# Softmax on one core: VectorE scales every row by its own scalar, ScalarE scales none

## The chip, the core and the metric

The kernel runs on one core of a Trainium2 chip. The engines that work here are VectorE (DVE in the profile), ScalarE (ACT), GpSimd (POOL) and SyncE (SP); SP, ACT and POOL also issue transfers, each into queues of its own, and the core's 16 DMA engines carry them. TensorE is idle. The metric is the device time of one execution in microseconds (us); lower is better. The kernel before takes 161.75 us, the median of 3 runs (161.74 to 161.76).

## What is computed

The input is a float32 tensor of 16 x 1024 x 512, 33.55 MB; the output has the same shape. It is a softmax over the last axis with temperature 0.5:

```python
x_scaled = x / 0.5
x_max = np.max(x_scaled, axis=-1, keepdims=True)
exp_x = np.exp(x_scaled - x_max)
return exp_x / np.sum(exp_x, axis=-1, keepdims=True)
```

## The kernel before

The 16384 rows of 512 elements are cut into 8 chunks of 2048 rows. A chunk is a tile `xt` of 128 partitions by 16 rows by 512 elements, 4 MB (4.19 million bytes). There are six such buffers (`BUFS = 6`), so chunk 6 uses chunk 0's buffer again, and chunk 7 chunk 1's. Everything is computed in place in the buffer.

*Transfers.* `load(c)` (L61, the transfer on L68) loads a chunk on SP's queue. Chunk 0 comes in two pieces of 4 and 12 rows, chunks 1 to 6 whole, and chunk 7 without its last row. That row is loaded by `load_last_row` (L88) on POOL's queue, as soon as a copy (L90) has seen ScalarE's sum of row 10 of chunk 5. The loads of chunks 0 to 5 wait for nothing but the queue; those of chunks 6 and 7 wait until stores 0 and 1 have landed. `store(i)` (L144, the transfer on L148) stores a whole chunk and is issued on ScalarE's queue, once all 16 rows have been scaled.

*Compute.* A chunk is worked on in blocks (`BLOCKS`): chunk 0 in blocks of 4, 4 and 8 rows, chunks 1 to 6 in one block of 16, chunk 7 in two of 8; 11 blocks in all. For one block:

- `shift(i)` (L71), VectorE: the negative row maxima of the whole block in one reduction (L77), then one tiny multiply by 2 gives the biases (L81).
- `exponentials(i, rows)` (L102), ScalarE: one activation per row (L108), exp(2x + bias), which also gives the row's sum.
- `scale_vector(i)` (L120), VectorE: the reciprocals of the block's sums (L125), and one multiply of the first seven eighths of the block's rows by them, the reciprocals being broadcast along each row (L127).
- `scale_scalar(i)` (L133), ScalarE: the last eighth of the rows, one activation per row (L138), Copy with the reciprocal as the per-partition scale. This is two rows of a block of 16, one of a block of 8, none of a block of 4.

*Order.* The schedule is written out by hand: each engine runs its instructions in the order in which the program names them. The loop over blocks (L163) names, for block i: the exponentials of block i+1 (for chunk 1 all but the last two rows), `scale_vector(i)`, `scale_scalar(i)`, the maxima and biases of block i+2, the store if the block ends a chunk, and then the rows of block i+1 that were left out. So VectorE alternates between scaling a block and reducing the block after next, and its next scale waits for ScalarE's exponentials of that block; ScalarE's exponentials wait for VectorE's biases. At the very end SP waits for what is listed in `finished` (L174).

Of the kernel before, what the change touches and what calls it, by code (L numbers as in the profile page):

```python
# [1 line left out]

# [4 lines left out]


@with_exitstack
def kernel(  # L10
    ctx: ExitStack,
    tc: tile.TileContext,
    x: bass.AP,
    out: bass.AP,
):
    nc = tc.nc
    fp32 = mybir.dt.float32
    P = nc.NUM_PARTITIONS
    AX = mybir.AxisListType.X
    EXP = mybir.ActivationFunctionType.Exp  # L20
    COPY = mybir.ActivationFunctionType.Copy
    MAX = mybir.AluOpType.max

    D = x.shape[-1]
    xf = x.flatten_outer_dims()
    of = out.flatten_outer_dims()
    N = xf.shape[0]

    G = 16
    C = N // (P * G)
    assert C * P * G == N
    xr = xf.rearrange("(c p g) d -> c p g d", p=P, g=G)
    outr = of.rearrange("(c p g) d -> c p g d", p=P, g=G)
    WHOLE = [(0, G)]
    LOADS = [[(0, 4), (4, G)]] + [WHOLE] * 6 + [[(0, G - 1)]]
    BLOCKS = [[(0, 4), (4, 8), (8, G)]] + [WHOLE] * 6 + [[(0, 8), (8, G)]]
    STORES = [WHOLE] * 8  # L40
    BMAX = 16
    BUFS = 6

    data = ctx.enter_context(tc.tile_pool(name="data", bufs=BUFS))
    stats = ctx.enter_context(tc.tile_pool(name="stats", bufs=6))

    ctx.enter_context(tc.manual_schedule())


    warm = stats.tile([P, 1], fp32, name="warm", bufs=1)  # L50
    nc.vector.memset(warm, 0.0)  # L51
    nc.scalar.activation(out=warm, in_=warm, func=EXP)  # L52

    chunks = {}
    blocks = [(c, lo, hi) for c in range(C) for lo, hi in BLOCKS[c]]
    n = len(blocks)
    biases, sums, recips = {}, {}, {}

    finished = []

    def load(c):  # L61
        if c < BUFS:
            chunks[c] = data.tile([P, G, D], fp32, name="xt")
        else:
            chunks[c] = chunks[c - BUFS]
        xt = chunks[c]
        for lo, hi in LOADS[c]:
            part = nc.sync.dma_start(out=xt[:, lo:hi, :], in_=xr[c][:, lo:hi, :])  # L68
            finished.append(part.ins.name)

    def shift(i):  # L71
        c, lo, hi = blocks[i]
        if c not in chunks:
            load(c)
        b = hi - lo
        negmax = stats.tile([P, BMAX], fp32, name="negmax")
        nc.vector.tensor_reduce(  # L77
            negmax[:, 0:b], chunks[c][:, lo:hi, :], axis=AX, op=MAX, negate=True
        )
        biases[i] = stats.tile([P, BMAX], fp32, name="bias")  # L80
        nc.vector.tensor_scalar_mul(biases[i][:, 0:b], negmax[:, 0:b], 2.0)  # L81

    def load_last_row(signal):  # L88
        seen = stats.tile([P, 1], fp32, name="seen", bufs=1)
        copied = nc.gpsimd.tensor_copy(out=seen, in_=signal)  # L90
        finished.append(copied.ins.name)
        c = C - 1
        halves = "p (h d) -> p h d"
        to = chunks[c - BUFS][:, G - 1, :].rearrange(halves, h=2)
        of_ = xr[c][:, G - 1, :].rearrange(halves, h=2)
        for p0, p1 in ((P - 2, P), (0, P - 2)):
            part = nc.gpsimd.dma_start(  # L97
                out=to[p0:p1], in_=of_[p0:p1], max_dma_last_dim=2 * D
            )
            finished.append(part.ins.name)  # L100

    def exponentials(i, rows):  # L102
        c, lo, hi = blocks[i]
        if i not in sums:
            sums[i] = stats.tile([P, BMAX], fp32, name="sums")
        for g in rows:
            row = chunks[c][:, lo + g, :]
            nc.scalar.activation(  # L108
                out=row,
                in_=row,  # L110
                func=EXP,
                bias=biases[i][:, g : g + 1],
                scale=2.0,
                accum_out=sums[i][:, g : g + 1],
            )
            if c == BUFS - 1 and g == 10:
                load_last_row(sums[i][:, g : g + 1])


    def scale_vector(i):  # L120
        c, lo, hi = blocks[i]
        b = hi - lo
        k = b - b // 8
        recips[i] = stats.tile([P, BMAX], fp32, name="recip")
        nc.vector.reciprocal(recips[i][:, 0:b], sums[i][:, 0:b])  # L125
        rows = chunks[c][:, lo : lo + k, :]
        last = nc.vector.tensor_mul(  # L127
            rows, rows, recips[i][:, 0:k].unsqueeze(2).broadcast_to((P, k, D))
        )
        if i == n - 1:  # L130
            finished.append(last.ins.name)

    def scale_scalar(i):  # L133
        c, lo, hi = blocks[i]
        b = hi - lo
        for g in range(b - b // 8, b):
            row = chunks[c][:, lo + g, :]
            last = nc.scalar.activation(  # L138
                out=row, in_=row, func=COPY, scale=recips[i][:, g : g + 1]
            )  # L140
            if i == n - 1:
                finished.append(last.ins.name)

    def store(i):  # L144
        c, _, end = blocks[i]
        for lo, hi in STORES[c]:
            if hi == end:
                part = nc.scalar.dma_start(  # L148
                    out=outr[c][:, lo:hi, :], in_=chunks[c][:, lo:hi, :]
                )  # L150
                if c < C - 1:
                    finished.append(part.ins.name)

    shift(0)
    shift(1)

    def rows(i):
        c, lo, hi = blocks[i]
        cut = hi - lo - (2 if c == 1 else 0)
        return range(cut), range(cut, hi - lo)  # L160

    exponentials(0, rows(0)[0])
    for i in range(n):  # L163
        if i + 1 < n:
            exponentials(i + 1, rows(i + 1)[0])
        scale_vector(i)
        scale_scalar(i)
        if i + 2 < n:
            shift(i + 2)
        store(i)  # L170
        if i + 1 < n:
            exponentials(i + 1, rows(i + 1)[1])

    seen = nc.sync.nop()  # L174
    info = mybir.DependencyInfo(
        mybir.DependencyClass.Sync, mybir.DependencyReason.DATA
    )
    for name in finished:
        tc.add_manual_dep(seen.ins, name, info, reason="leaves one wait for the end")


# [1 line left out]
_INS = ['x']  # L183
_OUTS = [((16, 1024, 512), 'float32')]


# [23 lines left out]
```

## Time and profile before

| quantity | value |
| --- | --- |
| median of 3 runs | 161.75 us |
| span of the profiled execution, first to last instruction | 160.5 us |
| VectorE busy | 134.6 us, 84% of the span, 45 instructions |
| ScalarE busy | 102.2 us, 64%, 273 instructions |
| DMA, whole span | 67.13 MB, mean 418 GB/s |
| a 16-row block on VectorE: maxima (L77) / scale of 14 rows (L127) | 8.68 / 7.62 us |
| a row on ScalarE: exponential (L108) / scale (L138) | 708 / 706 ns |

The page gives the span of the profiled execution; its time is not listed beside those of the three runs. Those lie 1.25 us above the span: what comes before the first instruction and after the last. 

When a store or a late load is issued, and when it lands (issue and time to landing are the trace's, the landing is their sum):

| transfer | issued, us | to landing, us | landed, us |
| --- | --- | --- | --- |
| store of chunk 0 | 44.10 | 24.5 | 68.6 |
| store of chunk 1 | 58.95 | 28.9 | 87.9 |
| store of chunk 2 | 75.57 | 31.4 | 107.0 |
| store of chunk 3 | 92.18 | 28.8 | 121.0 |
| store of chunk 4 | 108.81 | 21.7 | 130.5 |
| store of chunk 5 | 125.43 | 14.8 | 140.2 |
| store of chunk 6 | 133.00 | 17.0 | 150.0 |
| store of chunk 7 | 147.48 | 12.2 | 159.7 |
| load of chunk 6 | 68.67 | 27.6 | 96.3 |
| load of chunk 7, rows 0 to 14 | 88.02 | 27.8 | 115.8 |
| load of chunk 7, last row (POOL, two pieces) | 104.82 | 9.1 and 15.4 | about 120.9 |

How to read the profile's lines: a group of instructions is given as line, engine, operation, output and input with their shapes (partitions x elements) and a count; then busy time in us, the mean duration of one in ns, and the engine's idle time just before them with what ended it. A line of a timeline begins with start and duration in us. A line of busy times by stretch gives the stretch, its length, the busy time of VectorE, ScalarE and POOL in it, TensorE's granted clock, the share of the 16 DMA engines that was busy (packets are counted where they start, so short stretches can exceed 1), and GB/s. A line of a DMA queue gives packets, MB, and the time that its packets took as a share of 16 engines; q1 holds SP's loads, q10 ScalarE's stores, q0 POOL's load.

### The profile page before, as it was taken

The numbers are of one execution on the slowest core, as the hardware profiler recorded it, in microseconds if no ns is written. First come the engines' busy times: TensorE is split into PE (matmuls) and PEld (weight loads), VectorE is DVE, ScalarE is ACT, GpSimd is POOL, SyncE is SP. The second block draws the span as 40 slices with busy tenths as digits, with TensorE's granted clock in tenths as the row PEclk, the third lists the DMA queues.
The fourth block names the chain that finished last, engine by engine and source line by source line (L and its number), as shares of the span: only waits on it lengthen the run. The fifth ranks groups of instructions, "written<-read, shape, count | busy, mean of one in ns | idle before, by whom it ended". The sixth has DMA issues, their size and how long they took to land.

```text
span 160.5 us, 411 instructions
## 1 busy us (share of the span) xinstructions
DVE 134.6 (84%) x45; ACT 102.2 (64%) x273; POOL 1.9 (1%) x7
## 2 busy tenths in 40 slices
DVE  0607999999999999999999999999999999957000
ACT  3071549069989963998199909991899891790000
POOL 0000000000000000000000000030000000000000
DMA  5999999999989999999999999989999999999994
GB/s 184 470 408 498 400 392 457 457 392 402 506 269 425 490 392 400 506 400 392 490 425 392 474 434 392 490 383 483 422 450 400 400 465 441 392 457 449 400 441 204
DMA packets 2578, 67.13 MB, mean 418 GB/s; under 512 B 328, under 2 KB 328, under 8 KB 400
## 3 DMA queue, kind: packets, MB, share of 16 engines
q1 hardware_dynamic: 1296, 33.29, 49.3%
q10 hardware_dynamic: 1152, 33.55, 48.4%
q0 software_dynamic: 128, 0.26, 0.4%
q14 instruction: 2, 0.02, 0.0%
HBM read 33.55 MB, written 33.55 MB: 418 GB/s over the span
## 4 chain that ended last, share of the span: by engine, by line
DVE 75%; DMA 7%; issue 5%; ACT 3%; SPq 0%
DVE negmax L77 42%; DVE xt L127 31%; DMA xt<-in_x_dram 7%; ACT xt L108 3%; DVE bias L81 1%; DVE recip L125 1%; SPq L68 0%
## 5 line engine op out<-in xcount | busy, mean ns | idle before, releaser
L108 ACT ACTIVATE xt<-xt,bias 128x512 f32<-128x512 f32 x128 | 90.4, 708 | 41.5 <-DVE bias L81 40.6
L77 DVE TENSOR_REDUCE negmax<-xt 128x16 f32<-128x8192 f32 (+2 forms) x11 | 69.9, 6352 | 9.4 <-DMA xt<-in_x_dram 9.4
L127 DVE TENSOR_TENSOR xt<-xt,recip 128x7168 f32<-128x7168 f32 (+2 forms) x11 | 62.0, 5637 | 0.4
L108 ACT ACTIVATION_READ_ACCUMULATOR xt<-xt,bias 128x1 f32 x128 | 23.9, 187 | 0.0
L138 ACT ACTIVATE xt<-xt,recip 128x512 f32<-128x512 f32 x15 | 9.9, 706 | 0.0
L125 DVE RECIPROCAL recip<-sums 128x16 f32<-128x16 f32 (+2 forms) x11 | 2.4, 218 | 1.8 <-ACT xt L108 1.8
L81 DVE TENSOR_SCALAR bias<-negmax 128x16 f32<-128x16 f32 (+2 forms) x11 | 1.9, 173 | 0.4
L52 ACT ACT_TABLE_LOAD x1 | 1.3, 1283 | 0.7 <-PEq L194 0.7
L97 POOL DMA_DIRECT2D xt<-in_x_dram x2 | 1.5, 741 | 0.5 <-issue 0.5
L90 POOL COPY seen<-sums 128x1 f32<-128x1 f32 x1 | 0.2, 184 | 103.6 <-ACT xt L108 103.6
L51 DVE MEMSET warm<- 128x1 f32 x1 | 0.1, 59 | 0.8 <-PEq L194 0.8
L52 ACT ACTIVATE warm<-warm 128x1 f32<-128x1 f32 x1 | 0.2, 202 | 0.0
L194 POOL MEMSET const-float32-0.0<- 128x1 f32 x1 | 0.1, 93 | 0.2 <-issue 0.2
L194 POOL MEMSET const-bfloat16-1.0<- 128x1 bf16 x1 | 0.1, 95 | 0.0
L194 POOL MEMSET const-uint8-127<- 128x1 uint8 x1 | 0.1, 95 | 0.0
L194 POOL MEMSET const-float32-1.0<- 128x1 f32 x1 | 0.1, 93 | 0.0
## 6 DMA issues: line engine op xcount, KB each, us to landing
out_dram<-xt ACTq DMA_DIRECT2D x8, 4096.0 KB, 23.1
xt<-in_x_dram SPq DMA_DIRECT2D x6, 4096.0 KB, 34.8
xt<-in_x_dram SPq DMA_DIRECT2D x1, 3840.0 KB, 27.8
xt<-in_x_dram SPq DMA_DIRECT2D x1, 3072.0 KB, 11.6
xt<-in_x_dram SPq DMA_DIRECT2D x1, 1024.0 KB, 4.8
xt<-in_x_dram POOLq DMA_DIRECT2D x1, 252.0 KB, 15.4
xt<-in_x_dram POOLq DMA_DIRECT2D x1, 4.0 KB, 9.1
```

What stands on the lines that cost most here:

```text
L51: nc.vector.memset(warm, 0.0)
L52: nc.scalar.activation(out=warm, in_=warm, func=EXP)
L77: nc.vector.tensor_reduce(negmax[:, 0:b], chunks[c][:, lo:hi, :], axis=AX, op=MAX, negate=True)
L81: nc.vector.tensor_scalar_mul(biases[i][:, 0:b], negmax[:, 0:b], 2.0)
L90: copied = nc.gpsimd.tensor_copy(out=seen, in_=signal)
L97: part = nc.gpsimd.dma_start(out=to[p0:p1], in_=of_[p0:p1], max_dma_last_dim=2 * D)
L108: nc.scalar.activation(out=row, in_=row, func=EXP, bias=biases[i][:, g : g + 1], scale=2.0, accum_out=sums[i][:, g : g + 1],)
L125: nc.vector.reciprocal(recips[i][:, 0:b], sums[i][:, 0:b])
L127: last = nc.vector.tensor_mul(rows, rows, recips[i][:, 0:k].unsqueeze(2).broadcast_to((P, k, D)))
L138: last = nc.scalar.activation(out=row, in_=row, func=COPY, scale=recips[i][:, g : g + 1])
L194: nc = _bacc.Bacc("TRN2", target_bir_lowering=False, num_devices=1)
```

## The change

VectorE's one broadcast multiply per block is replaced by one multiply per row, whose second operand is a per-partition scalar, the row's reciprocal; it covers all rows of the block. ScalarE scales no rows. The reciprocal, the order of the loop and all transfers stay as they are named; `finished` is created some lines earlier, without effect. The lines of the code after move up by a few (the row multiply is L126 there, the store L134).

```diff
-    def scale_vector(i):
+    def scale(i):
         c, lo, hi = blocks[i]
         b = hi - lo
-        k = b - b // 8
         recips[i] = stats.tile([P, BMAX], fp32, name="recip")
         nc.vector.reciprocal(recips[i][:, 0:b], sums[i][:, 0:b])
-        rows = chunks[c][:, lo : lo + k, :]
-        last = nc.vector.tensor_mul(
-            rows, rows, recips[i][:, 0:k].unsqueeze(2).broadcast_to((P, k, D))
-        )
+        for g in range(b):
+            row = chunks[c][:, lo + g, :]
+            last = nc.vector.tensor_scalar_mul(row, row, recips[i][:, g : g + 1])
         if i == n - 1:
             finished.append(last.ins.name)
-
-    def scale_scalar(i):
-        c, lo, hi = blocks[i]
-        b = hi - lo
-        for g in range(b - b // 8, b):
-            row = chunks[c][:, lo + g, :]
-            last = nc.scalar.activation(
-                out=row, in_=row, func=COPY, scale=recips[i][:, g : g + 1]
-            )
-            if i == n - 1:
-                finished.append(last.ins.name)
...
-        scale_vector(i)
-        scale_scalar(i)
+        scale(i)
```

VectorE's instructions go from 45 to 162: 11 multiplies leave, 128 come. ScalarE loses 15 activations. The multiplies of a block wait once, the first of them, for the reciprocals; the others follow without a wait. A store waits for VectorE's last multiply alone.

More of the change, by code (lines that the diff above doesn't have):

```diff
@@ L20 @@
     EXP = mybir.ActivationFunctionType.Exp
-    COPY = mybir.ActivationFunctionType.Copy
     MAX = mybir.AluOpType.max
@@ L54 @@
     chunks = {}
+    finished = []
     blocks = [(c, lo, hi) for c in range(C) for lo, hi in BLOCKS[c]]
@@ L57 @@
     biases, sums, recips = {}, {}, {}
-    finished = []
     def load(c):
```

## The prediction

> **What bounds the kernel now.** I first read the chain of work that ended last, because it names a suspect:
>
> ```profile
> span 160.5 us, 411 instructions
> DVE 134.6 (84%) x45; ACT 102.2 (64%) x273; POOL 1.9 (1%) x7
> DVE 75%; DMA 7%; issue 5%; ACT 3%; SPq 0%
> DVE negmax L77 42%; DVE xt L127 31%; DMA xt<-in_x_dram 7%; ACT xt L108 3%; DVE bias L81 1%; DVE recip L125 1%; SPq L68 0%
> ```
>
> It says VectorE: row maxima and the scaling edited here. But the chain is followed back from the last instruction, and the last store lands 12.2 us after that instruction issues it. So next the DMA view from 2 to 159 us, and the busy times in stretches:
>
> ```profile
> DMA packets 2558, 67.02 MB, mean 427 GB/s; under 512 B 321, under 2 KB 321, under 8 KB 393
> q1 hardware_dynamic: 1283, 33.19, 50.0%
> q10 hardware_dynamic: 1145, 33.55, 49.5%
> q0 software_dynamic: 128, 0.26, 0.4%
> ```
>
> ```profile
> 2.00:22.00 20.00, 11.58 (x7) 6.08 (x18) 0.00 (x0) 1.00 1.02 437
> 62.00:82.00 20.00, 19.86 (x8) 15.07 (x41) 0.00 (x0) 1.00 1.00 431
> 122.00:142.00 20.00, 19.34 (x8) 14.89 (x40) 0.00 (x0) 1.00 1.00 433
> 142.00:159.00 17.00, 4.09 (x2) 2.46 (x6) 0.00 (x0) 1.00 0.96 414
> ```
>
> The queues' shares add to 50.0 + 49.5 + 0.4 = 99.9% of the sixteen engines' time over 157 us. The share (the column before GB/s) is about 1 where only loads run, where loads and stores mix, and where only stores are left. All of the input and output must pass; there is no idle time to squeeze out. **The transfers are the bound, and VectorE's chain runs just fast enough to feed them.** How closely shows at the end:
>
> ```profile
> 125.28 7.62 DVE L127 TENSOR_TENSOR xt<-xt,recip 128x7168 f32<-128x7168 f32 x1
> 132.83 4.41 DVE L77 TENSOR_REDUCE negmax<-xt 128x8 f32<-128x4096 f32 x1
> 143.27 0.20 DVE L125 RECIPROCAL recip<-sums 128x8 f32<-128x8 f32 x1 [1.79 <-ACT xt L108]
> 143.50 3.89 DVE L127 TENSOR_TENSOR xt<-xt,recip 128x3584 f32<-128x3584 f32 x1
> 147.48 0.34 ACTq L148 DMA_DIRECT2D out_dram<-xt  x1
> ```
>
> The last five stores land at about 121.0, 130.5, 140.2, 150.0 and 159.7 us, 9.5 to 9.8 us apart, though they are issued 16.6, 16.6, 7.6 and 14.5 us apart: the queue is always full and drains at its own pace. The last store is issued 2.5 us before its predecessor lands, and the first load, issued at 0.74 us, shows its first traffic after 1.7, some 1 to 1.2 us later. So the margin is at most about 1.3 us; I take 1.2. An earlier store only queues longer; one later by more than that opens a hole.
>
> **The change, part by part.** Removed: eleven broadcast multiplies (L127) and fifteen ScalarE rows (L138). Added: 128 multiplies of one 512-element row. Prices:
>
> ```profile
> L127 DVE TENSOR_TENSOR xt<-xt,recip 128x7168 f32<-128x7168 f32 x6 | 45.7, 7625 | 0.2
> L127 DVE TENSOR_TENSOR xt<-xt,recip 128x3584 f32<-128x3584 f32 x3 | 11.7, 3892 | 0.1
> L127 DVE TENSOR_TENSOR xt<-xt,recip 128x2048 f32<-128x2048 f32 x2 | 4.6, 2292 | 0.1
> L81 DVE TENSOR_SCALAR bias<-negmax 128x16 f32<-128x16 f32 x6 | 1.0, 174 | 0.2
> L81 DVE TENSOR_SCALAR bias<-negmax 128x8 f32<-128x8 f32 x3 | 0.5, 171 | 0.1
> L81 DVE TENSOR_SCALAR bias<-negmax 128x4 f32<-128x4 f32 x2 | 0.3, 170 | 0.1
> ```
>
> *The multiply goes:* (7625 − 3892)/3584 = 1.042 ns per element plus 159 ns fixed.
> *The row multiply comes:* its nearest row is L81, the same operation with a constant for the column scalar: 170, 171 and 174 ns for 4, 8 and 16 elements. That is 4 ns over 12 elements, 0.33 each, where the multiply's slope would give 12.5. So this operation passes more than one element per step. Low end: 174 + 496 × 0.33 = 338 ns. High end, the multiply's slope: 174 + 496 × 1.042 = 691 ns. I take half that slope, the whole fraction nearest to 4 in 12: 174 + 258 = 432 ns. VectorE starts an independent instruction about 85 ns before the earlier one's recorded end (bias to reciprocal 0.08 us apart with 0.17 recorded; 132.83 against 125.28 + 7.62), so rows follow at 0.253, **0.347** or 0.606 us.
>
> The Trainium skill, "VectorE: DVE Perf Modes", section "The perf-mode tier table", gives fp32 tensor_scalar from SBUF two results a cycle and tensor_tensor one; the L81 and L127 slopes agree in direction, and no row here shows a 512-element tensor_scalar. By its 58 + FD/Accel cycles a row would take an estimated 0.327 us, a chunk 5.2 us. The same page's "Rules for kernel authors" speaks against the change, asking for fewer operations; by it the 117 added instructions cost what they save only if the faster mode fails.
>
> *A chunk:* 16 × 0.347 + 0.085 = 5.64 us against 7.62 (ends 4.13 and 9.78). The scales on VectorE's path are two of 4 rows, two of 8 and six of 16 (the third 8-row scale lies beside the last exponentials): before 2 × 2.29 + 2 × 3.89 + 6 × 7.62 = 58.1 us; after 120 × 0.347 + 0.85 = 42.5 us. Equal at (58.1 − 0.85)/120 = 0.477 us per row.
>
> *ScalarE's rows go:* 9.9 us off an engine that idles 40.6 us on biases (L81); the cover is that idle time. The 0.9 us in two waits on its own scaling goes too. Each store, on ScalarE's queue, now waits only for VectorE's last row. Behind it stand the next exponentials. A chunk's scale (5.6 us) runs beside 16 exponentials (11.3 us), so ScalarE does not stop; beside chunk 7's first 8 exponentials (5.6 us) it may wait 0.2 us, and the next exponentials await a later bias anyway.
>
> *Instruction supply:* VectorE has 117 more instructions, ScalarE 15 fewer. The trace's two instruction fetches (queue 14, 0.02 MB) show no stall behind them; a third would be 0.01 MB, and VectorE's lead at the end covers a few us of waiting. Costed at nothing.
>
> *What moves:* the exponentials before store 0 start 2 × (2.29 − 1.47) = 1.64 us earlier and the 0.71 us scale behind them goes: store 0 issues 2.3 us earlier, near 41.8. It then takes half of the traffic from the loads, so chunk 7's load lands up to 2.3 us later, 115.8 + 2.3 = 118.1. SP's loads of chunks 6 and 7 (waiting for stores 0 and 1) go out earlier, behind loads still queued. POOL's load of chunk 7's last row starts when its ScalarE signal does, also earlier.
>
> *Is every store in time?* The bytes are the same, so once the loads are through the stores can land as before, at 130.5 (store 4), 140.2, 150.0 and 159.7, if each is issued by 1.3 us before its predecessor lands: store 5 by 129.2, store 6 by 138.9, store 7 by 148.7. Store 5 follows chunk 6's exponentials: landed near 98.6 (96.3 + 2.3), maxima 8.7, bias 0.2, exponentials 11.3, so near 119. Store 6: 118.1 + 4.4 (maxima) + 0.4 + 5.6 (scale) = 128.5. Store 7: 128.5 + 4.4 + 0.2 + 5.8 (eight exponentials) + 0.2 + 2.9 (eight rows) = 142.0, 5.5 us earlier than now and 6.7 before it is due. No hole opens, and nothing changes at the end of the traffic. What is late next, on VectorE, are the loads of chunks 6 and 7.
>
> *Sum:* span 160.5 + 0 = 160.5 us. The three runs have a median of 161.75, so 1.25 us lies around the span and stays: **161.75 us**.
>
> **The rivals.**
> *Slower: the row runs at one element per step.* For it: no row shows a 512-element row or a pointer scalar. Against: L81's slope. At 0.606 the path grows to 120 × 0.606 + 0.85 = 73.6 us, 15.5 more; less the margin of 1.2 it ends near 161.75 + 14.3 = 176 us. It decides from (58.1 + 1.2 − 0.85)/120 = 0.487 us per row on. Chance 9%.
> *Slower: POOL's last row of chunk 7 is late.* It now lands 15.4 us after issue, near 120.9, and is needed near 128.5. It decides only from 128.5 + 6.7 = 135.2 on. Held until the end of chunk 6's scale and landing 15.4 us later, it comes at 143.9, and the end 8.7 us late, near 170.5. Against: its signal comes 11 exponentials after chunk 4's scale may start, 7.7 us, when a 5.6 us scale is over. The skill's "SBUF — State Buffer", section "Who interferes with whom", has a two-port VectorE operation hold GpSimd off, descriptors too; before has no such long operation, so no row shows it. Chance 3%.
> *Faster: the chain is the real bound.* Then 5.5 us come off: 156.25. For it: 75% of the chain. Against: 67.02 MB in 157 − 5.5 us need 442 GB/s, over the mean of 427 at full shares and over the last stores' 4.19 MB per 9.7 us = 432. Chance 2%; another 2% for transfers a little quicker in another order.
>
> **How the numbers follow.** Hidden: 84%, 161.75 us, own range 161.55 to 161.95 (0.1% each way; the three runs differ by 0.02). Slower 12%, faster 4%, by the bound of 0.2% (0.32 us), about what a measurement of this kernel can tell from no change. The range of 161.45 to 162.1 holds the hidden case; both rivals' sizes lie outside with 16%.
>
> **What would show it.** Right: row multiplies near 0.43 us recorded and 0.35 apart, VectorE's total near 134.6 − 62.0 + 128 × 0.432 = 128 us of overlapping records, new VectorE waits for loads of chunks 6 and 7, last store issued between 139 and 143, DMA shares again 99.9%, last stores 9.7 us apart. Wrong: rows over 0.48 us apart, VectorE without waits, a DMA hole before the last store, or chunk 7's last maxima waiting for POOL's row.

## The result, and the profile after

The changed kernel takes 162.50 us (median of 6 runs, 162.17 to 162.68), the kernel before 161.75 us beside it (6 runs, 161.72 to 162.10): a ratio of 1.0039, with a 95% interval of 1.0026 to 1.0052. (The ratios here and below are those on record; the ratio of two medians can lie about 0.1% off them.) It is slower by 0.4%; the medians lie 0.75 us apart. The prediction said no change, 161.75, and its range ended at 162.1.

The page of the changed kernel, whose profiled execution took 162.48 us:

```profile
span 160.7 us, 508 instructions
DVE 124.5 (77%) x162; ACT 92.9 (58%) x258; POOL 1.9 (1%) x7
DMA 51%; DVE 31%; ACT 8%; issue 1%; DVEq 0%; SPq 0%
L107 ACT ACTIVATE xt<-xt,bias 128x512 f32<-128x512 f32 x128 | 90.4, 708 | 49.9 <-DVE bias L80 23.2
L126 DVE TENSOR_SCALAR xt<-xt,recip 128x512 f32<-128x512 f32 x128 | 51.7, 481 | 0.4
```

Both engines got the time that the change was to give them: VectorE is busy 10.1 us less than before, ScalarE 9.3 us less. The chain that ended last, 75% VectorE before, is now 51% DMA. Yet the kernel is slower, so the time isn't on either engine. The DMA view from 2 to 159 us, and the busy times in the same four stretches as before (columns: stretch, length, VectorE, ScalarE, GpSimd, clock, share of the DMA engines, GB/s):

```profile
DMA packets 2564, 67.04 MB, mean 427 GB/s; under 512 B 325, under 2 KB 325, under 8 KB 397
q1 hardware_dynamic: 1284, 33.19, 49.8%
q10 hardware_dynamic: 1149, 33.55, 49.6%
q0 software_dynamic: 128, 0.26, 0.4%
q14 instruction: 3, 0.02, 0.0%
```

```profile
2.00:22.00 20.00, 11.53 (x13) 6.45 (x19) 0.00 (x0) 1.00 1.03 437
62.00:82.00 20.00, 19.77 (x31) 15.93 (x46) 0.00 (x0) 1.00 1.01 434
122.00:142.00 20.00, 18.95 (x30) 10.39 (x30) 0.00 (x0) 1.00 1.01 436
142.00:159.00 17.00, 3.46 (x9) 1.54 (x6) 0.00 (x0) 1.00 0.96 412
```

The queues still add to 49.8 + 49.6 + 0.4 = 99.8%, and no stretch shows a hole. That reading of the bound held. The one line with a new count is the smallest: queue 14, which fetches instructions, has three packets of 8 KB in place of two, and its share rounds to nothing. The experiments below ask whether this line is the one that costs.

The VectorE timeline answers to the end of the chain before:

```profile
111.14 6.42 DVE L126 TENSOR_SCALAR xt<-xt,recip 128x512 f32<-128x512 f32 x16
121.92 4.42 DVE L76 TENSOR_REDUCE negmax<-xt 128x8 f32<-128x4096 f32 x1 [4.35 <-DMA xt<-in_x_dram]
126.73 6.42 DVE L126 TENSOR_SCALAR xt<-xt,recip 128x512 f32<-128x512 f32 x16
143.57 0.20 DVE L123 RECIPROCAL recip<-sums 128x8 f32<-128x8 f32 x1 [2.48 <-ACT xt L107]
143.81 3.26 DVE L126 TENSOR_SCALAR xt<-xt,recip 128x512 f32<-128x512 f32 x8
```

Sixteen rows take 6.42 us, eight 3.26: (6.42 − 3.26)/8 = 0.395 us apart, with 0.48 recorded. A chunk's scale saves 7.62 − 6.42 = 1.2 us. But the maxima of chunk 7 wait 4.35 us for their load, which landed at 121.9, and so the last store is issued at 147.10, only 0.4 us earlier than in the profile of before. ScalarE's timeline shows why the load is late:

```profile
37.88 0.71 ACT L107 ACTIVATE xt<-xt,bias 128x512 f32<-128x512 f32 x1
38.00 0.38 ACTq L134 DMA_DIRECT2D out_dram<-xt  x1
38.49 0.19 ACT L107 ACTIVATION_READ_ACCUMULATOR xt<-xt,bias 128x1 f32 x1
38.58 0.71 ACT L107 ACTIVATE xt<-xt,bias 128x512 f32<-128x512 f32 x1
...
147.10 0.34 ACTq L134 DMA_DIRECT2D out_dram<-xt  x1
```

Store 0 is issued at 38.00 us, in the middle of the exponentials of chunk 1, of which the program names fourteen before it. Before, it came at 44.10, after ScalarE's own scale, for which it waited. Now it overtakes five of the fourteen, which start only at 38.58 us and later. VectorE's last multiply of chunk 0 ended at 35.59, so the store didn't go out at once when VectorE was done; the next five stores too are issued when five of the sixteen exponentials named before them have yet to start. Store 0 so takes half of the traffic from the loads 6.1 us earlier, not the 2.3 us that I had worked out.

### The profile page after: what moved, and what is told of

The parts are those of the page before. It is cut to its first block, busy times and chain, and to the rows that moved or that the text cites. A ratio compares the mean times of both kernels' runs of the same rounds, so it can differ in the third digit from the quotient of the medians.

```text
span 160.7 us, 508 instructions
## 1 busy us (share of the span) xinstructions
DVE 124.5 (77%) x162; ACT 92.9 (58%) x258; POOL 1.9 (1%) x7
## 4 chain that ended last, share of the span: by engine, by line
DMA 51%; DVE 31%; ACT 8%; issue 1%; DVEq 0%; SPq 0%
DMA xt<-in_x_dram 32%; DVE negmax L76 20%; DMA out_dram<-xt 19%; DVE xt L126 10%; ACT xt L107 8%; DVE bias L80 1%; DVE recip L123 1%; DVEq L190 0%; SPq L67 0%
## 5 line engine op out<-in xcount | busy, mean ns | idle before, releaser
L126 DVE TENSOR_SCALAR xt<-xt,recip 128x512 f32<-128x512 f32 x128 | 51.7, 481 | 0.4
## 6 DMA issues: line engine op xcount, KB each, us to landing
xt<-in_x_dram POOLq DMA_DIRECT2D x1, 252.0 KB, 21.3
```

Of the source, the lines that this page charges most:

```text
L126: last = nc.vector.tensor_scalar_mul(row, row, recips[i][:, g : g + 1])
```

## The experiments

Three theories stood at first, and the expectations name them. **A**: VectorE's longer instruction stream costs, whatever the instructions do. **B**: the earlier stores make the last load, and with it the last store, only barely in time. **C**: the row multiply itself, beside the transfers. Out of A came later A1 (one more fetch of 8 KB of instructions holds back one DMA engine) and A2 (each instruction costs a little).

| run | what it is | us, this / before beside it | ratio (95%) | span of the profiled execution, us | fetches on queue 14 during the run, at us |
| --- | --- | --- | --- | --- | --- |
| e0_before | the kernel before | 161.92 / 161.84 | 1.0005 (0.9991–1.0018) | 160.0 | 37.5, 96.9 |
| after | the change | 162.50 / 161.75 | 1.0039 (1.0026–1.0052) | 160.7 | 36.3, 51.6, 96.2 |
| e1_pad | before + 117 idle instructions, VectorE | 162.54 / 161.83 | 1.0041 (1.0025–1.0056) | 160.9 | 6.6, 38.7, 98.1 |
| e5_pad40 | before + 40, VectorE | 161.92 / 161.84 | 1.0002 (0.9991–1.0013) | 160.0 | 19.3, 37.4, 96.8 |
| e12_pad48 | before + 48, VectorE | 162.27 / 161.94 | 1.0023 (1.0009–1.0036) | 160.4 | 6.6, 38.7, 98.1 |
| e8_pad65 | before + 65, VectorE | 162.38 / 161.95 | 1.0019 (1.0005–1.0033) | 160.4 | 6.6, 38.6, 97.9 |
| e9_pad95 | before + 95, VectorE | 162.35 / 161.95 | 1.0024 (1.0011–1.0036) | 160.6 | 6.7, 38.7, 97.9 |
| e6_poolpad | before + 120, GpSimd, at the start | 162.56 / 161.84 | 1.0042 (1.0025–1.0058) | 161.4 | 6.6, 37.6, 97.2 |
| e11_poollate | before + 120, GpSimd, later | 162.00 / 161.94 | 1.0009 (0.9998–1.0021) | 160.2 | 33.8, 37.6, 96.9 |
| e7_both | e1 and e6 together | 162.45 / 161.84 | 1.0035 (1.0023–1.0046) | 160.8 | 6.6, 6.6, 38.7, 98.2 |
| e2_ts14 | row multiplies for 7/8, ScalarE the rest | 162.71 / 161.83 | 1.0049 (1.0033–1.0065) | 161.0 | 36.3, 51.6, 92.1 |
| e3_gate | after, with the order of the stores as before | 162.47 / 161.83 | 1.0039 (1.0027–1.0052) | 160.7 | 36.1, 51.9, 92.1 |
| e4_tt16 | broadcast multiply of all rows, VectorE | 169.19 / 161.83 | 1.0466 (1.0427–1.0506) | 167.0 | 37.3, 96.9 |
| e10_mix | half broadcast, half by rows, VectorE | 165.70 (its two shortest runs of six; 167.91 over all six) / 161.95 | 1.0228 (1.0194–1.0261) | 166.9 | 37.6, 67.4, 91.7 |
| e13_mixgate | e10, with the order as before | 162.43 / 161.94 | 1.0032 (1.0021–1.0043) | 160.9 | 37.5, 66.3, 96.1 |

### Idle instructions alone: e1_pad

```diff
+    extra = stats.tile([P, 117], fp32, name="extra", bufs=1)
+    for k in range(60):
+        nc.vector.memset(extra[:, k : k + 1], 0.0)
     shift(0)
+    for k in range(60, 117):
+        nc.vector.memset(extra[:, k : k + 1], 0.0)
     shift(1)
```

> The kernel before, with 117 one-column memsets on VectorE added in its first two idle stretches (60 before the first maxima, 57 before the second); nothing else is changed, so VectorE has the 162 instructions of the changed kernel and the scales of the kernel before. Theory A, the 0.75 us come from VectorE's longer instruction stream, mostly as time around the span: time around the span 1.7 to 1.8 us instead of 1.25, total near 162.3. Theory B, they come from stores that are issued earlier and so a last load and a last store that are barely in time: no change, 161.7 to 161.8. Theory C, they come from the row multiply itself beside the transfers: no change, 161.7 to 161.8.

The kernel before with as many VectorE instructions as after (162). They write zeros to a tile that nobody reads, while VectorE waits for its first two loads. The page of this run, VectorE's timeline, and the DMA view from 6 to 8 us:

```profile
span 160.9 us, 528 instructions
DVE 137.4 (85%) x162; ACT 102.2 (64%) x273; POOL 1.9 (1%) x7
```

```profile
0.84 1.72 DVE L156 MEMSET extra<- 128x1 f32 x60
5.46 2.29 DVE L77 TENSOR_REDUCE negmax<-xt 128x4 f32<-128x2048 f32 x1 [2.90 <-DMA xt<-in_x_dram]
7.89 1.15 DVE L159 MEMSET extra<- 128x1 f32 x57
13.40 2.29 DVE L77 TENSOR_REDUCE negmax<-xt 128x4 f32<-128x2048 f32 x1 [4.36 <-DMA xt<-in_x_dram]
```

```profile
q1 hardware_dynamic: 32, 0.79, 92.9%
q14 instruction: 1, 0.01, 1.0%
```

The idle instructions end 2.90 and 4.36 us before the loads that VectorE waits for anyway: by running they cost VectorE nothing. The kernel is slower by 0.41%, as much as the change makes it. So a loss of this size comes without a single row multiply and with the stores ordered as before. What the two kernels share are 117 more VectorE instructions and one fetch more.

They are not alike in all. The fetch at 6.6 us falls into the load of chunk 0's second piece, and the maxima that wait for this load start at 13.40 us. In e0_before (below; the kernel before, unchanged) they start at 12.69, and VectorE carries the delay to the end. First e0_before's maxima and last store, then e1_pad's last store:

```profile
12.69 2.29 DVE L77 TENSOR_REDUCE negmax<-xt 128x4 f32<-128x2048 f32 x1 [4.79 <-DMA xt<-in_x_dram]
147.37 0.34 ACTq L148 DMA_DIRECT2D out_dram<-xt  x1
```

```profile
148.07 0.34 ACTq L148 DMA_DIRECT2D out_dram<-xt  x1
```

The last store goes out 0.7 us later, late enough that most DMA engines, followed one by one as below, stand idle for 0.1 to 0.3 us near 149 us. The changed kernel has neither the delay nor the pause: its second maxima start at 12.78 us, and its added fetch comes at 51.6. So a fetch at 6.6 us may cost in two ways, by the DMA engine that carries it and by VectorE's later chain.

### The number of instructions, or the fetch: e0_before, e5_pad40, e6_poolpad, e7_both

e0_before is the kernel before, unchanged, as a measure of what no change looks like.

> The kernel before, unchanged, to see its span beside its own time. In the changed kernel and in the runs made so far the time lies 1.73 to 1.82 us above the span of the same execution. If that is a constant, the profiled execution of before with its span of 160.5 took about 162.3 and was not one of those near 161.75; this one then has a time 1.77 us above its span. If the time around the span depends on the kernel, it is 1.25 us here.

e5_pad40 has 40 idle instructions, all ahead of the first maxima:

```diff
+    extra = stats.tile([P, 40], fp32, name="extra", bufs=1)
+    for k in range(40):
+        nc.vector.memset(extra[:, k : k + 1], 0.0)
     shift(0)
```

> The kernel before with 40 one-column memsets on VectorE before the first maxima. VectorE then has some 93 rows in the trace, 53 before. Theory A1 (an added 8 KB fetch of instructions during the run holds back the one DMA engine that carries it, and the slowest engine ends the run): if the fetch comes once an engine has run about 50 rows, as ScalarE's first (after 50 or 51 rows) and VectorE's (after 50 to 64), there are three fetches and the time is near 162.5; if it comes only for a stream of over 128, there are two and the time is near 161.8. Theory A2 (each added instruction costs a little): 161.8 + 40/117 of 0.7 = 162.05. Theory B (work of VectorE itself is late): 161.8.

e6_poolpad gives 120 to GpSimd, which has nothing to do there, and e7_both has the additions of e1_pad and of e6_poolpad:

```diff
+    idle = stats.tile([P, 120], fp32, name="idle", bufs=1)
+    for k in range(120):
+        nc.gpsimd.memset(idle[:, k : k + 1], 0.0)
     shift(0)
```

> The kernel before with 120 one-column memsets on GpSimd at the start, where it is idle; VectorE and ScalarE are as before. Theory A1: a third fetch during the run, now GpSimd's, and 162.4 to 162.6. Theory A2, if any engine's instructions cost: the same; if only VectorE's do: 161.8.

> Both paddings, 117 memsets on VectorE and 120 on GpSimd. Theory A1: four fetches; if all are carried by the same DMA engine, that engine ends about 0.3 to 0.7 us later again, 162.9 to 163.2; if the two added fetches fall on different engines, near 162.5 as with one. Theory B: 161.8.

The GpSimd instructions cost the same 0.42%, on an engine that takes part in one late load only. So it is not VectorE's instruction count. But the fetch at 6.6 us holds up VectorE's chain here too: the second maxima start at 13.10 us and the last store at 147.78, against 12.69 and 147.37 in e0_before. Both paddings together cost no more than one (1.0035); by the reading of single engines below, their two added fetches fall on two different engines. Forty instructions cost nothing, but they didn't spare the fetch, as the page of e5_pad40 shows; it came later, as its DMA view from 19 to 20.5 us has it:

```profile
span 160.0 us, 451 instructions
DVE 135.7 (85%) x85; ACT 102.2 (64%) x273; POOL 1.9 (1%) x7
q14 instruction: 3, 0.02, 0.0%
```

```profile
q1 hardware_dynamic: 19, 0.62, 98.4%
q14 instruction: 1, 0.01, 1.3%
```

Three fetches, and the span of the kernel before, 160.0 us. "One fetch more is 0.4%" was too simple.

### When the fetch comes: e8_pad65, e9_pad95, e12_pad48, e11_poollate

The first three change the 40 of e5_pad40 to 65, 95 and 48.

> The kernel before with 65 one-column memsets on VectorE before the first maxima: 118 rows in its trace, so its 50th row is run near 4 us and its third fetch comes near 6 us, as with 117 memsets, but the stream stays under 128 rows. If the fetch and its early time make the loss: near 162.5. If it takes a stream of more than 128 rows: 161.8 to 161.95, as with 40.

> The same with 95 memsets: 148 rows, over 128, one fetch, near 6 us. If a stream of more than 128 rows makes the loss: near 162.5, like 117 memsets. If each row costs a little: 161.84 + 95/117 of 0.7 = 162.4; with 65, 162.2.

> The kernel before with 48 memsets on VectorE before the first maxima instead of 40: 101 rows instead of 93, but the 50th is now run before 6 us, so that the added fetch should come near 6.6 us instead of 19.3. If the fetch's time decides: 162.3 to 162.5. If the number of rows does: 161.9, as with 40.

e11_poollate holds the 120 GpSimd instructions of e6_poolpad until ScalarE has summed the last row of chunk 0:

```diff
+        if i == 1:
+            idle = stats.tile([P, 121], fp32, name="idle", bufs=1)
+            nc.gpsimd.tensor_copy(out=idle[:, 120:121], in_=sums[2][:, 7:8])
+            for k in range(120):
+                nc.gpsimd.memset(idle[:, k : k + 1], 0.0)
         scale_vector(i)
```

> The kernel before with 120 memsets on GpSimd as in the earlier padding of GpSimd, but held back until ScalarE has summed row 7 of chunk 0's last block, so that GpSimd's 50th row is run near 30 us instead of before 7. If any added fetch on a busy DMA engine costs, wherever it falls: near 162.5. If what costs is that it falls into chunk 0's load, near 6.6 us, as in all paddings that were slower: 161.8 to 161.95.

Eight more instructions, 48 for 40, move the fetch from 19.3 to 6.6 us and turn 1.0002 into 1.0023. The same 120 GpSimd instructions with the fetch at 33.8 in place of 6.6 us cost 1.0009 in place of 1.0042. So for these paddings the time of the fetch decides; the intervals of the GpSimd pair lie apart, those of the VectorE pair overlap a little. With the later fetches VectorE's chain is in time as well: the last store is issued at 147.52 us in e5_pad40 and 147.34 in e11_poollate, against 148.06 in e12_pad48 and 147.78 in e6_poolpad. From 48 to 95 the loss doesn't grow (1.0023, 1.0019, 1.0024), which speaks against A2; the 1.0041 of 117 lies higher, but the intervals overlap.

To see what a fetch does, I followed the packets in the trace engine by engine: on one DMA engine the next packet starts 3 to 4 ns before the recorded end of the one before. A sequence from the changed kernel (start in us, duration in ns, queue, bytes), and what the sixteen engines end with (the last packet's end, in us):

```
after, one engine:    50.37 1213 q10 32768 | 51.58 309 q14 8192 | 51.89 1751 q1 32768 | 53.64 1213 q10 32768
e0_before, one engine: 36.33 1213 q1 32768 | 37.53 309 q14 8192 | 37.84 1578 q1 32768 | 39.42 1218 q1 32768

engine's end     without a fetch     ScalarE's two fetches    the added fetch
e0_before        157.97 to 158.66    158.74                   none
e5_pad40         158.12 to 158.77    158.63                   158.87
e11_poollate     157.94 to 159.01    158.75                   158.80
e1_pad           158.67 to 158.88    158.82                   159.76
e12_pad48        158.66 to 158.82    158.88                   159.21
e6_poolpad       158.38 to 158.63    160.22                   159.47
e13_mixgate      157.65 to 159.07    159.05                   159.68
after            158.37 to 159.33    159.26                   159.21
e2_ts14          157.77 to 159.65    159.02                   159.66
e3_gate          157.88 to 159.02    158.86                   159.42
```

A fetch takes 0.31 us of one engine, and the packet behind it takes 1.58 or 1.75 us in place of 1.21: together 0.7 to 0.85 us on one engine of sixteen. No other engine takes that over, since each has its own sixteenth of every transfer, and the last store is complete only with the last of them. The span goes with that last engine: it ends 1.1 to 1.4 us after it in every row of the table. That the two fetches of the kernel before (ScalarE's, going by its count of instructions; the trace names no engine) cost nothing has a reason there: they fall on one of the two engines that carry 2 KB or less of chunk 7's late row, where the other fourteen mostly carry 18, and so it ends level with the rest. In e1_pad the engine with the added fetch ends 0.9 us after all others and has no pause near 149 us; the others end 158.67 to 158.88, not much later than in e0_before. By this reading the engine, and not VectorE's later chain, makes most of e1_pad's loss in the profiled execution (162.71 us).

How far an engine lies behind the middle one of the sixteen, both taken when they have moved the same bytes, also tells why an early fetch can be free. It puts its engine 0.5 to 1.2 us behind. When store 0 begins, packets of 1.4 us and more come on every engine, and part of the lag is given back. At about 62 us the engine with the added fetch is 0.44 us behind in e5_pad40 and 0.34 in e11_poollate, which lose nothing clear of noise, and 0.60 to 1.12 us in the paddings with a fetch at 6.6 us. The fetches at 51.6 to 51.9 us (after, e2_ts14, e3_gate) come behind this point; their engine is 0.66 to 0.75 us behind at 62 us, and 0.57 to 1.10 near the end.

The Trainium skill, "DMA: Bandwidth & Descriptors", section "Two DMAs through the same engine are not ordered", says that nothing orders transfers across the sixteen engines; the ends above, up to 2.0 us apart in one kernel, agree.

Not all is settled. In the changed kernel three engines end late (159.21, 159.26, 159.33), and the last of them had no fetch; in e2_ts14 one without a fetch ends level with the one that had it. In e6_poolpad the engine with ScalarE's two fetches is last, and it had those before; that profile is of one of its longer executions (163.2 us, the median is 162.56). Why more of the lag is given back after a fetch at 19.3 or 33.8 us than after one at 6.6, the runs don't say. And every run with an added fetch after store 0 has row multiplies too, so that for the changed kernel no run separates the fetch from theory C; for the fetch speaks that its engine falls behind by 0.8 us just where it comes, in after, e2_ts14, e3_gate and e13_mixgate alike. The assignment of packets to engines is my reconstruction from start and end times, not a column of the trace; where packets of two engines end together it can exchange the two, as in e5_pad40, where 158.63 could also be 158.71.

### The row multiply without the other half of the change: e2_ts14

```diff
-        rows = chunks[c][:, lo : lo + k, :]
-        last = nc.vector.tensor_mul(
-            rows, rows, recips[i][:, 0:k].unsqueeze(2).broadcast_to((P, k, D))
-        )
+        for g in range(k):
+            row = chunks[c][:, lo + g, :]
+            last = nc.vector.tensor_scalar_mul(row, row, recips[i][:, g : g + 1])
```

> One part of the change alone: VectorE scales by row multiplies, but only the seven eighths of the rows that it had before; ScalarE scales its two rows of sixteen as before, so each store is again issued behind ScalarE's own scale. VectorE has 147 instructions. Theory A: near 162.3, with 1.7 to 1.8 us around the span. Theory B: the stores are back behind ScalarE's exponentials, the last load is near its old 116 us, 161.7 to 161.8. Theory C: 113 of 128 row multiplies remain, near 162.4.

ScalarE keeps its eighth, so the stores keep their place: store 0 at 42.95 us, the last at 141.51, 6 us earlier than before. The kernel is as slow as after, 1.0049, with its added fetch again at 51.6 us. B falls with it: the last store is in time by far. C is not touched: 113 of the 128 row multiplies are in this kernel.

### The order of the stores: e3_gate

```diff
             if hi == end:
+                spot = chunks[c][:, hi - 1, 0:1]
+                nc.scalar.activation(out=spot, in_=spot, func=COPY)
                 part = nc.scalar.dma_start(
```

> The changed kernel with one tiny ScalarE copy in place (one element per partition of the chunk's last row, multiplied by nothing) ahead of each store, so that the store is issued only when ScalarE has worked off the exponentials in front of it, as before. Theory A: near 162.5, around the span 1.7 to 1.8 us. Theory B: store 0 issues near 43 instead of 38.0, chunk 7's load lands near 117 to 118 instead of 121, and the time is back at 161.7 to 161.9. Theory C: near 162.5.

A copy of one element per partition on ScalarE, onto itself, ahead of each store of the changed kernel, puts the store behind the exponentials again. ScalarE's timeline around store 0 and the last store:

```profile
42.01 0.19 ACT L136 ACTIVATE xt<-xt 128x1 f32<-128x1 f32 x1
42.22 0.38 ACTq L137 DMA_DIRECT2D out_dram<-xt  x1
142.31 0.34 ACTq L137 DMA_DIRECT2D out_dram<-xt  x1
```

Store 0 comes at 42.22 and the last store at 142.31, within some 0.4 us of the 41.8 and 142.0 that the prediction had worked out. The time stays at 162.47, a ratio of 1.0039. So this kernel does what was predicted of the stores, and is 0.4% slower all the same; an earlier last store buys nothing, as predicted, and the order of the stores isn't the cause of the loss.

### The other half of the change: e4_tt16, and a mixture: e10_mix, e13_mixgate

e4_tt16 does the part of the change that takes the rows off ScalarE, with the multiply of before:

```diff
-        rows = chunks[c][:, lo : lo + k, :]
+        rows = chunks[c][:, lo:hi, :]
         last = nc.vector.tensor_mul(
-            rows, rows, recips[i][:, 0:k].unsqueeze(2).broadcast_to((P, k, D))
+            rows, rows, recips[i][:, 0:b].unsqueeze(2).broadcast_to((P, b, D))
         )
...
-        scale_scalar(i)
```

> The other part alone: ScalarE scales none, VectorE scales all rows with the broadcast multiply. Per 16-row block 8.69 us instead of 7.62 on VectorE's path, 1.07 more six times and 0.53 more twice, so the last store is issued 7.5 us later, less ScalarE's 0.1 at the end, less the margin of 1.2 us: near 161.75 + 6.3 = 168 on every theory. It tells what ScalarE's two rows were worth. Time around the span: 1.25 us by theory A, since VectorE has 45 instructions.

It takes 169.19 us, 4.7% more and 1.2 us over the 168 expected. VectorE's multiplies grow from 62.0 to 70.0 us, on an engine that had no time to give. Its store 0 overtakes the exponentials too, at 39.13 us, and its last store comes at 155.00.

e10_mix was meant to beat both kernels: all rows on VectorE, half of a chunk's by the broadcast multiply and half by rows, so that the instruction stream stays shorter than after (104 VectorE instructions); e13_mixgate adds e3_gate's copy.

```diff
-        for g in range(b):
+        single = {0: 0, 1: 0, n - 2: 0, n - 1: 4}.get(i, 8)
+        for g in range(single):
             row = chunks[c][:, lo + g, :]
             last = nc.vector.tensor_scalar_mul(row, row, recips[i][:, g : g + 1])
+        if single < b:
+            rows = chunks[c][:, lo + single : hi, :]
+            last = nc.vector.tensor_mul(
+                rows,
+                rows,
+                recips[i][:, single:b].unsqueeze(2).broadcast_to((P, b - single, D)),
+            )
```

> The change with a short instruction stream: VectorE scales all rows and ScalarE none, as in the changed kernel, but in each block of 16 only eight rows singly and the other eight by one broadcast multiply (0.395 us a row and 0.533), 112 rows in the trace. VectorE's path: 2 x 2.29 + 3.2 + 6 x 7.55 + 3.9 = 57.0 us, against 58.1 before and about 48.6 in the changed kernel, so the last store should go out about 1 us earlier than in the kernel before. If a stream of more than 128 rows makes the loss: 161.8 to 162.0 though ScalarE scales nothing. If taking the scaling from ScalarE, or the row multiply itself, makes it: near 162.5.

> The short mixture of single rows and a broadcast multiply, with the tiny ScalarE copy ahead of each store, so that a store is issued behind ScalarE's exponentials again. If the mixture lost its 6 us because its stores overtook ScalarE's exponentials and so pushed chunk 7's load to 126.9 us: store 0 issues near 43, chunk 7's load lands near 116 to 118, the last store issues near 147 and the time is 161.9 to 162.6. If the loss is in the mixture's own work: 167 to 168.

It beat neither. Without the copy its six runs take 165.14 to 168.67 us, with it seven take 162.17 to 162.78: here the order of the stores is worth some 3 us, going by the two shortest runs without it (165.14 and 166.25), which the ratio in the table is taken from. The profile of e10_mix is of the longest of its six runs (168.67; the shortest took 165.14), so its lines show the kind of loss, not its size. First, of e10_mix, the timeline with stores 0 and 7 and the first maxima of chunk 7, and its stretch from 140 to 160 us; then the same two stores and stretch of e13_mixgate:

```profile
39.21 0.38 ACTq L142 DMA_DIRECT2D out_dram<-xt  x1
127.29 4.42 DVE L76 TENSOR_REDUCE negmax<-xt 128x8 f32<-128x4096 f32 x1 [4.47 <-DMA xt<-in_x_dram]
154.25 0.34 ACTq L142 DMA_DIRECT2D out_dram<-xt  x1
```

```profile
140.00:160.00 20.00, 12.81 (x10) 5.75 (x16) 0.00 (x0) 1.00 0.76 326
```

```profile
43.56 0.38 ACTq L145 DMA_DIRECT2D out_dram<-xt  x1
146.86 0.34 ACTq L145 DMA_DIRECT2D out_dram<-xt  x1
```

```profile
140.00:160.00 20.00, 5.24 (x7) 2.59 (x9) 0.00 (x0) 1.00 0.91 393
```

Store 0 at 39.21 lets the loads get half of the traffic from then on, and chunk 7's load lands at 127.3 (121.9 after, 115.8 before). VectorE, slower here than after, has no lead left to make up for it; the last store comes at 154.25, and the DMA engines have a hole: 0.76 of their time against 0.91. In the changed kernel the same overtaking cost 5 us of VectorE's lead (147.10 against e3_gate's 142.31) and no time. By the engine-by-engine reading a single engine, the one with ScalarE's fetches, carries chunk 7's load to 126.9 us where the other fifteen are through by 119.9; in e4_tt16 it is the same, 125.9 against 120.7. Why that engine falls so far behind when stores start early stays open.

## Why the prediction was wrong

*The bound.* Right. The transfers' share stayed at 99.8%, 10 us less on VectorE and 9 us less on ScalarE brought nothing, and e3_gate's 5 us earlier last store brought nothing over after.

*The row multiply.* Right in kind, mis-sized. It does pass more than one element per step, against the first rival (0.606 us apart); but rows come 0.396 us apart (6.42/16 is 0.401 with the tail of the last row) and not 0.347, and record 481 ns and not 432. A chunk takes 6.42 us for 5.64 predicted. The break-even of 0.487 wasn't reached. By the Trainium skill, "VectorE: DVE Perf Modes", section "The TRN2 errata", 58 + FD/Accel cycles make an estimated 0.327 us for a row; the trace has 0.07 more, and decides.

*ScalarE's rows.* Right that they bring nothing; they had cover before. e2_ts14, which leaves them on ScalarE, has 1.0049 against 1.0039, with intervals that overlap.

*What moves.* The step "store 0 issues 2.3 us earlier, near 41.8" was wrong for the changed kernel. It took it for granted that the store stays behind the exponentials named before it. What had held it there was its wait for ScalarE's own scale, and that went with the scale. Store 0 came at 38.00, chunk 7's load at 121.9 (predicted 118.1), the last store at 147.10 (predicted 142.0, due 148.7). The margin shrank from the expected 6.7 us to 1.6. It was still kept, so this error cost the prediction no time; in e10_mix, with a slower VectorE, the same thing costs some 3 us.

*Is every store in time?* Right: no hole, though barely. The due date of 148.7 was too late by about a microsecond: in e1_pad and e12_pad48 a last store at 148.06 or 148.07 already came after a pause on most DMA engines, while the 147.10 of the changed kernel came before any.

*Instruction supply.* This is the step that failed: "a third would be 0.01 MB, and VectorE's lead at the end covers a few us of waiting. Costed at nothing." I saw the third fetch coming and priced it as a mean over sixteen engines and as a wait on VectorE. It is neither. The kernel before already had the sign: "no stall behind them" holds for the compute engines, but the packet behind its fetch at 37.5 us took 1.58 us in place of 1.21. In the sequences followed it takes 0.7 to 0.85 us of one DMA engine, in a kernel where all sixteen are full from start to end, and the end is that of the slowest. Shown is that idle instructions alone, on VectorE or GpSimd, cost 0.41 and 0.42% when their fetch comes at 6.6 us and nothing clear of noise when it comes at 19.3 or 33.8, so that the term can't be put at nothing. That the held-back engine is what costs rests on the reading of single engines: it is clear in e1_pad and e3_gate, where this engine ends last by 0.9 and 0.4 us, and less so in the changed kernel itself, where an engine without a fetch ends as late. How much of the changed kernel's 0.4% is the fetch stays open; it lies neither in VectorE's time nor in the order of the stores.

*The time around the span.* "1.25 us lies around the span" was wrong by a comparison of unlike executions. In the runs where both are known it is 1.72 to 1.83 us (after 162.48 − 160.7, e0_before 161.74 − 160.0). The profile of before with its span of 160.5 was thus of an execution of about 162.3 us, longer than the median by half a microsecond. By like executions the spans are 160.0 and 160.7, and the difference is the measured one.

*The rivals.* None came. The larger piece of GpSimd's late row, the second of two issued from 100.12 us on, landed 21.3 us after its issue, near 122.1, before its maxima started at 133.07; no run shows GpSimd held off by VectorE's row multiplies, which the Trainium skill, "SBUF — State Buffer", section "Who interferes with whom", describes for operations that use both ports. A slower case without a late store was missing among the rivals, since I took everything that isn't on the chain or in the bytes as free.

## What to carry to other kernels

When all DMA engines are full from the first load to the last store, the end is that of the slowest one, and what takes one engine aside can count, though it needn't: added instructions are among it, and a line that rounds to 0.0% can be worth 0.4%. Less time on an engine that has cover is worth nothing there, but more instructions may cost; an added padding that does no work is the quick way to find that out. Where an edit takes the last compute instruction ahead of a transfer off the issuing engine, look for what else held the transfer in its place, and ask what it does to the other transfers if it goes early.

## What the runs showed of the hardware

- Instructions are fetched while the kernel runs, 8 KB at a time, by the same DMA engines that carry its data (as the packets, followed engine by engine, have it): 0.31 us of one engine, and 0.37 to 0.54 us more for the packet behind it in the two sequences shown. The fetch came at 6.6 us with 48 idle instructions at the start, at 19.3 with 40.
- A transfer issued from ScalarE's queue runs ahead of activations named before it, when it waits for none of them: issued at 38.00 us, with five of the fourteen exponentials named before it yet to start; these went on to 42.1. The next five stores of the changed kernel were also five exponentials ahead. One activation over a single column (0.19 us, e3_gate) holds it back.
- Row multiplies with a per-partition scalar on 128 x 512 float32 come 0.396 us apart and record 0.48; the broadcast multiply takes 1.04 ns per element, or 0.53 us for as many elements.
